# A gated DeltaNet layer on one core: adaLN slices 0 and 1 shared by two engines, and the first norms placed later in TensorE's order

## Chip, cores and metric

The kernel runs on 1 core of one Trainium2 chip. A time is the device time of one execution in microseconds (us). The kernel before takes 1131.63 us, the median of 3 runs (1130.09 to 1136.4).

## The reference

One decoder layer (DEPTH = 1) for a sequence of 1024 tokens of width 1024 in float32: adaLN modulation, a gated DeltaNet mixer, a gated residual and a last RMSNorm.

```python
mod = silu(c) @ ada_w + ada_b                       # 1024 x 3072
shift, scale, gate = split(mod, 3)
h = rms_norm(x, norm_g) * (1 + scale) + shift
proj = h @ w_in                                     # q, k, v, z, beta, a
q, k, v = silu(causal_conv4(proj_qkv))              # then q, k normalised per head
# per chunk of 64 tokens and head: A = strict_lower(beta k k^T * decay); T = (A + I)^-1
# u = T (v beta), w = T (k beta exp(gc)); a scan over the chunks carries the state
o = rms_norm(o, norm_w) * silu(z)
out = rms_norm(x + gate * (o @ w_out), final_g)
```

16 value heads share 8 query/key heads; a head has 128 channels. The kernel works with chunks of 128 tokens and 8 groups of two value heads.

## The kernel before

**Prologue (L356 to L418).** x comes in 8 row tiles. For each, ScalarE sums squares (`x_stat`), VectorE scales by the inverse norm (`x_scale`), TensorE transposes (`x_turn`, two halves of four blocks) and ScalarE or VectorE copies the result out of PSUM into `xT`: VectorE, but for the first half of the tiles in `EV_ACT`. The adaLN shift and scale are made in 8 slices of 128 channels. `ada_load(i)` brings slice i of `ada_w` (k = 0 to 7, shift and scale, two DMAs of 512 KB). Of the eight k, `ada(i)` (L233) adds up the first `KV[i]` on VectorE, one operation of 256 elements for each; `modulate(i)` (L245) does the rest on TensorE as matmuls with one moving column (L250) and folds in the accumulator with a matmul against ones (L253). With `KV[i] = 0` everything is TensorE's. Then VectorE makes the columns shift and scale (L254 to L257), ScalarE applies them to the slice's 128 rows of `xT` in two halves (L260) and makes the high part (L262), and GpSimd makes the low part (L263). Each float32 product is made of three products of high and low parts.

`first_w` and `first_lo` load and split three weight tiles: 0 is k of head 0, 1 is q of head 0, 2 is the beta and a columns. `first_project(i, j, hf)` adds channel slice i of weight tile j for token half hf into its own PSUM bank; the list `units` holds what is still to be done and `drain(n)` does n of it. `keep_warm(n)` issues n matmuls of constants.

The order of TensorE, VectorE, ScalarE and GpSimd is written out by hand in the prologue (`manual_schedule`). SP issues the DMAs of x, `ada_w` and the weights.

**Groups (L947 and on).** From here only TensorE's order is given by hand; the others' order is a planner's. `drive` mixes streams (generators that yield a cost and a delay until they are due again, in ns of a virtual clock) with filler (projection matmuls at `MM` = 216 each): a stream that is due goes first, otherwise one filler matmul is issued; when the filler is used up, the clock jumps to the next due time. Before group 0 (`gi = -1`) the streams are `gates` (second part, due at `D_G`), `stage_a(0)` (due at `START`) and `norms(1)` (due at `START1`). The filler is `proj_kq(1)`, 96 matmuls, and `values(0)` with three z heads, 240 more. `stage_a(0)` first runs `norms(0)`: for each token half transposes of k and q (L508, L515) into the two banks of tag `tr`, whose squares ScalarE sums in place (L512, L518), with `D_N` between the halves. After a delay `D_A0` follow eight Gram matmuls (L549), `D_A` apart; VectorE makes the matrices `at` from them (L551, L553). They go through DRAM into `ua`, VectorE solves 32 x 32 blocks in 31 steps (L575, L577), the result goes through DRAM into `TT`, VectorE transposes blocks of it (L597 to L599), and `levels` joins them in four TensorE steps (L603, L613, L622, L628), due `D_L0` after the Gram matmuls. Then group 0 begins with its scan.

Of the kernel before, what the change touches and what calls it, by code (L numbers as in the profile page):

```python
# [9 lines left out]
F32 = mybir.dt.float32  # L10
# [3 lines left out]
ALU = mybir.AluOpType  # L14
# [6 lines left out]

XB, WB = 8, 3
WA0 = 7
EV_ACT = (0, 1, 3, 5)
KV = (0, 0, 6, 6, 6, 6, 6, 7)
WARM = 14
PRE = (3, 5)
ND, ND0 = 3, 2

# [6 lines left out]
TURN = 40  # L36
MM = 216

START, START1 = 11000, 65000
D_G, D_RG = 9500, 11000  # L40
D_N, D_A0, D_A = 3000, 1500, 1000
D_L0, D_L1, D_L2, D_L3 = 46000, 1600, 1800, 1600
D_R, D_V, D_S = 500, 1100, 700
D_F0, D_F = 8000, 2000
# [3 lines left out]
def gdn_layer(ctx: ExitStack, tc: tile.TileContext, x, c, ada_w, ada_b, norm_g, w_in, conv_w, a_log, dt_bias,  # L48
# [8 lines left out]
    nc = tc.nc  # L57
# [7 lines left out]
    NHALF = T // TH  # L65
# [119 lines left out]
    def keep_warm(n):  # L185

        warm = bank("tr")
        for _ in range(n):
            nc.tensor.matmul(warm[:, :P], lhsT=ones, rhs=ident, start=True, stop=True)
# [26 lines left out]
    def ada_load(i):  # L216
        wa = q0.tile([P, KT, 2, P], F32, name="wa", tag="wa", bufs=WB)
        for s in range(2):
            nc.sync.dma_start(out=wa[:, :, s], in_=av[:, :, s, i])
        was[i] = wa  # L220
# [12 lines left out]
    def ada(i):  # L233

        wa, n = was[i], KV[i]
        if n == 0:
# [27 lines left out]
                                    h_hi[hf][i // 4][:, i % 4].bitcast(F32), op=ALU.subtract)  # L264

    first = [(8 * P, P), (0, P), (BA0, 2 * HV)]
    w0, acc0 = [], []

    v3 = lambda a: a.rearrange("p (n h) -> p n h", h=HV)

# [50 lines left out]
        yield 650, 0  # L321

    GENG = {nc.tensor.engine, nc.vector.engine}
    raw0 = []
    dtb = const.tile([P, HV], F32, name="dtb")
    nea = const.tile([P, HV], F32, name="nea")
    nc.scalar.dma_start(out=dtb, in_=dt_bias[0:1, :].to_broadcast([P, HV]))
# [2 lines left out]
    def first_w(j, load=False):  # L330
        c0, m = first[j]
        if load:
            raw = q0.tile([P, D], F32, name="w0raw", tag="xt", bufs=XB)[:, :KT * m].rearrange("p (k n) -> p k n", n=m)
            nc.sync.dma_start(out=raw, in_=wv[:, :, c0:c0 + m])
            raw0.append(raw)
            return
        both = q0.tile([P, KT, 2, m], F32R, name=f"w0{j}")
        nc.scalar.copy(both[:, :, 0], raw0[j])
        w0.append(both)

    def first_lo(j):
        hi, lo = w0[j][:, :, 0], w0[j][:, :, 1]
        nc.vector.tensor_tensor(lo, raw0[j], hi.bitcast(F32), op=ALU.subtract)
        w0[j] = (hi, lo) if j < 2 else w0[j].rearrange("p k s m -> p k (s m)")

    def first_project(i, j, hf):
# [10 lines left out]
    with tc.manual_schedule(engines={nc.tensor.engine, nc.vector.engine, nc.scalar.engine, nc.gpsimd.engine}):  # L357
# [3 lines left out]
        for t in range(NT):  # L361
            x_load(t)
            if t == WA0:
                ada_load(0)
        for j in range(3):
            first_w(j, True)
        for i in (1, 2):
            ada_load(i)
        for t in range(3):
            x_stat(t)  # L370
        x_scale(0)
        for t in range(NT):
# [6 lines left out]
                columns()  # L379
            if t + 3 < NT:  # L380
                x_stat(t + 3)
        first_w(1)
        first_w(2)
        first_lo(0)
        modulate(0)
        keep_warm(WARM)
        first_lo(1)
        first_lo(2)
        units = []

        def drain(n):
# [3 lines left out]
        for i in range(KT):  # L395
            if i + 3 < KT:
                ada_load(i + 3)
            if i > 0:
                drain(ND)
                if i + 1 < KT:  # L400
                    modulate(i + 1)
                if i + 2 < KT:
                    ada(i + 2)
                drain(1)
            for hf in range(NHALF):
                first_project(i, 2, hf)
            units += [(i, j, hf) for hf in range(NHALF) for j in range(2)]
            if i == 0:
                drain(ND0)
                modulate(1)  # L410
                ada(2)
                nc.scalar.activation(nea, nea, AF.Exp)
            if i in PRE:
                c0 = (9, 1)[PRE.index(i)] * P
                ahead[c0] = load_w(c0, P, wpool)
# [118 lines left out]
    def stage_a(gi, G):  # L534
# [3 lines left out]
            yield from norms(gi, G)  # L538
        D1 = dram.tile([16, P, 32], F32, name="D1", tag="D1", bufs=2)
        D2 = dram.tile([16, 4, 16, 2, 32], F32, name="D2", tag="D2", bufs=2)  # L540
        yield 0, D_A0
        for hf in range(NHALF):
            em, brk = G.em[hf], G.brk[hf]

# [491 lines left out]
```

## Time and profile before

| | us |
|---|---|
| median of 3 runs | 1131.63 |
| profiled execution | 1130.95 |
| its span | 1129.2 |

| engine | busy us | share of the span |
|---|---|---|
| TensorE (PE) | 1059.3 | 94% |
| weight loads (PEld) | 857.6 | 76% |
| VectorE (DVE) | 745.1 | 66% |
| ScalarE (ACT) | 536.6 | 48% |
| GpSimd (POOL) | 450.0 | 40% |

A busy share is an average over stages. Matmuls are pipelined and their ends are modelled, so a busy TensorE may be at half clock or running one-column matmuls; the granted clock (PEclk, 1.00 is 2.4 GHz and 0.50 is 1.2 GHz) tells one of the two, the forms in the timeline the other. A wait in brackets is idle time of the engine before the piece, with what ended it.

### The profile page before, as it was taken

The numbers are of one execution on the slowest core, as the hardware profiler recorded it, in microseconds if no ns is written. First come the engines' busy times: TensorE is split into PE (matmuls) and PEld (weight loads), VectorE is DVE, ScalarE is ACT, GpSimd is POOL, SyncE is SP. The second block draws the span as 40 slices with busy tenths as digits, with TensorE's granted clock in tenths as the row PEclk, the third lists the DMA queues.
The fourth block names the chain that finished last, engine by engine and source line by source line (L and its number), as shares of the span: only waits on it lengthen the run. The fifth ranks groups of instructions, "written<-read, shape, count | busy, mean of one in ns | idle before, by whom it ended". The sixth has DMA issues, their size and how long they took to land.

```text
span 1129.2 us, 18338 instructions
## 1 busy us (share of the span) xinstructions
PE 1059.3 (94%) x6295; PEld 857.6 (76%) x6295; DVE 745.1 (66%) x1914; ACT 536.6 (48%) x1416; POOL 450.0 (40%) x532
## 2 busy tenths in 40 slices
PE   8997999989999799999999999999899989999997
PEld 7875787767878678777877887788678768778785
DVE  5468775776579857865786677677766866513515
ACT  6567442453642455435543644364546424534523
POOL 3452223532444135323532452155216334954643
PEclk9998999999999999999999999999999989999999
DMA  9803333341145313421531143125313571446442
GB/s 287 234 19 133 75 82 85 101 126 43 39 135 164 83 50 100 125 56 30 145 102 45 42 146 84 39 54 163 74 29 103 149 219 63 140 135 185 152 121 75
DMA packets 188131, 119.48 MB, mean 106 GB/s; under 512 B 59733, under 2 KB 166534, under 8 KB 187014
## 3 DMA queue, kind: packets, MB, share of 16 engines
q1 hardware_dynamic: 187536, 118.20, 37.2%
q8 instruction: 50, 0.82, 0.3%
q14 instruction: 43, 0.35, 0.1%
q10 hardware_dynamic: 502, 0.10, 0.0%
HBM read 93.03 MB, written 25.24 MB: 105 GB/s over the span
## 4 chain that ended last, share of the span: by engine, by line
PE 41%; DVE 18%; ACT 6%; POOL 5%; DMA 4%; issue 4%; SPq 0%; POOLq 0%; DVEq 0%; ACTq 0%
PE pj L459 16%; PE pj L837 5%; DVE tb L577 4%; DVE tm L575 4%; DVE vT L446 3%; DVE em L497 3%; PE tr L549 2%; PE tr L837 2%; PE ts L755 2%; PE ks L736 1%; PE oq L709 1%; PE oq L762 1%; PE tr L622 1%; PE ks L767 1%; PE tr L628 1%
## 5 line engine op out<-in xcount | busy, mean ns | idle before, releaser
L124 POOL TENSOR_TENSOR wlo<-wraw,whi 128x512 fp32r<-128x512 f32 x92 | 126.1, 1379 | 147.3 <-ACT whi L123 107.7
L446 DVE SCALAR_TENSOR_TENSOR vT<-xb,taps,vT 128x512 f32<-128x512 f32 x96 | 84.6, 882 | 24.3 <-ACT vT L444 23.3
L446 DVE SCALAR_TENSOR_TENSOR kq<-xb,taps,kq 128x512 f32<-128x512 f32 x96 | 78.7, 828 | 12.9 <-ACT kq L444 11.0
L123 ACT CAST whi<-wraw 128x512 fp32r<-128x512 f32 x92 | 55.5, 618 | 64.9 <-PE pj L459 59.0
L577 DVE TENSOR_TENSOR tb<-tb,tm 128x126 f32<-128x126 f32 (+22 forms) x248 | 80.1, 323 | 4.8
L698 POOL TENSOR_TENSOR oT<-oT,z 128x256 f32<-128x256 f32 x64 | 50.6, 792 | 81.2 <-ACT oT L697 74.0
L575 DVE TENSOR_TENSOR tm<-tb,ua 128x126 f32<-128x126 f32 (+22 forms) x248 | 78.3, 316 | 6.2 <-DMA ua<-D 1.1
L459 PE MATMUL pj<-h1hia,whi 128*128 128x512 f32 x184 | 75.8, 412 | 6.6 <-ACT vT L444 6.6
L697 ACT ACTIVATE oT<-pot,cols 128x256 f32<-128x256 f32 x64 | 30.4, 474 | 108.1 <-PE pot L695 54.8
L459 PE MATMUL pj<-h0lob,whi 128*128 128x512 f32 x184 | 78.2, 425 | 0.0
L459 PE MATMUL pj<-h0hia,whi 128*128 128x512 f32 x184 | 76.8, 417 | 1.3 <-ACT kq L444 1.3
L459 PE MATMUL pj<-h1hib,whi 128*128 128x512 f32 x184 | 77.8, 423 | 0.0
L459 PE MATMUL pj<-h1lob,whi 128*128 128x512 f32 x184 | 77.7, 422 | 0.0
L459 PE MATMUL pj<-h1hia,wlo 128*128 128x512 f32 x184 | 77.5, 421 | 0.0
L459 PE MATMUL pj<-h0hib,wlo 128*128 128x512 f32 x184 | 77.1, 419 | 0.0
L459 PE MATMUL pj<-h1hib,wlo 128*128 128x512 f32 x184 | 76.6, 416 | 0.0
L459 PE MATMUL pj<-h0hia,wlo 128*128 128x512 f32 x184 | 75.8, 412 | 0.0
L459 PE MATMUL pj<-h1loa,whi 128*128 128x512 f32 x184 | 75.7, 411 | 0.0
L459 PE MATMUL pj<-h0loa,whi 128*128 128x512 f32 x184 | 75.6, 411 | 0.0
L459 PE MATMUL pj<-h0hib,whi 128*128 128x512 f32 x184 | 75.5, 410 | 0.0
L439 POOL MEMSET xb<- 128x3 f32 x32 | 3.4, 109 | 172.3 <-DVE kq L446 85.9
L719 POOL TENSOR_TENSOR sso<-sso,neg_half 128x2 f32<-128x2 f32 x64 | 44.6, 696 | 58.3 <-DVE sso L718 57.6
(445 smaller groups left out, 2933.1 us busy)
## 6 DMA issues: line engine op xcount, KB each, us to landing
wraw<-in_gdn_w_in SPq DMA_DIRECT2D x92, 256.0 KB, 2.9
woraw<-in_gdn_w_out SPq DMA_DIRECT2D x54, 256.0 KB, 3.2
wa<-in_ada_w SPq DMA_DIRECT2D x16, 512.0 KB, 6.9
em<-gc_dram SPq DMA_DIRECT2D x8, 1024.0 KB, 6.4
z_dram<-sz SPq DMA_DIRECT2D x32, 256.0 KB, 2.1
z<-z_dram SPq DMA_DIRECT2D x64, 128.0 KB, 2.4
o_dram<-oT SPq DMA_DIRECT2D x64, 128.0 KB, 1.9
gsrc<-o_dram SPq DMA_DIRECT2D x32, 256.0 KB, 2.9
```

The lines of the kernel that those rows point to most:

```text
L123: nc.scalar.copy(hi, raw)
L124: nc.gpsimd.tensor_tensor(lo, raw, hi.bitcast(F32), op=ALU.subtract)
L446: nc.vector.scalar_tensor_tensor(dst, xb[:, j:j + TH], tp[:, j], dst, op0=ALU.mult, op1=ALU.add)
L459: nc.tensor.matmul(ps[:m], lhsT=a[:, k, :m], rhs=b[half][k // 4][:, k % 4], start=(k == 0 and n == 0), stop=(k == KT - 1 and n == 2))
L497: nc.vector.scalar_tensor_tensor(em[:, h, n], em[:, h, n], ngc[:, n, h0 + h:h0 + h + 1], mask, op0=ALU.add, op1=ALU.add)
L549: nc.tensor.matmul(pg2[:, 0:2], lhsT=kq[hf][:, 0, js], rhs=kq[hf][:, :, js], start=True, stop=True)
L575: nc.vector.tensor_tensor(tmv, tb[:, :mm, j:j + 1].to_broadcast([P, mm, ln]), ua[:, j:j + 1, j + 1:].to_broadcast([P, mm, ln]), op=ALU.mult)
L577: nc.vector.tensor_tensor(tb[:, :mm, j + 1:], tb[:, :mm, j + 1:], tmv, op=ALU.subtract)
L697: nc.scalar.mul(oT, pot, normw_c)
L698: nc.gpsimd.tensor_tensor(oT, oT, zs.pop(n), op=ALU.mult)
L719: nc.gpsimd.tensor_tensor(sso, sso, neg_half[:, :2], op=ALU.pow)
L837: nc.tensor.matmul(acc, lhsT=a[:, ts], rhs=b, start=(first and n == 0), stop=(last and n == 2))
```

## The change

Constants: three k of slice 0 and five k of slice 1 go to VectorE (none before), slices 2 to 6 give it seven instead of six; the first halves of x tiles 6 and 7 are copied by ScalarE; the warm-up behind slice 0 has 10 matmuls instead of 14; `D_G` goes from 9500 to 11000, `START` from 11000 to 16000, and group 0 alone gets a `D_A0` of 6000 instead of 1500. Order: weight tile 1 (q) is loaded behind slice 1 of `ada_w`; `ada(0)` stands before `modulate(0)`, `first_lo` of tiles 0 and 2 behind it, then `ada(1)`, and tile 1 is split last, its low part by GpSimd; `units` lists both halves of k before those of q.

```diff
-EV_ACT = (0, 1, 3, 5)
-KV = (0, 0, 6, 6, 6, 6, 6, 7)
-WARM = 14
+EV_ACT = (0, 1, 3, 5, 6, 7)
+KV = (3, 5, 7, 7, 7, 7, 7, 7)
+WARM = 10
...
-START, START1 = 11000, 65000
-D_G, D_RG = 9500, 11000
-D_N, D_A0, D_A = 3000, 1500, 1000
+START, START1 = 16000, 65000
+D_G, D_RG = 11000, 11000
+D_N, D_A0, D_A = 3000, (6000, 1500), 1000
...
-        nc.vector.tensor_tensor(lo, raw0[j], hi.bitcast(F32), op=ALU.subtract)
+        (nc.gpsimd if j == 1 else nc.vector).tensor_tensor(lo, raw0[j], hi.bitcast(F32), op=ALU.subtract)
...
-        for j in range(3):
+        for j in (0, 2):
             first_w(j, True)
-        for i in (1, 2):
-            ada_load(i)
+        ada_load(1)
+        first_w(1, True)
+        ada_load(2)
...
-        first_w(1)
+        ada(0)
         first_w(2)
-        first_lo(0)
         modulate(0)
         keep_warm(WARM)
+        first_lo(0)
+        first_lo(2)
+        ada(1)
+        first_w(1)
         first_lo(1)
-        first_lo(2)
...
-            units += [(i, j, hf) for hf in range(NHALF) for j in range(2)]
+            units += [(i, j, hf) for j in range(2) for hf in range(NHALF)]
...
-        yield 0, D_A0
+        yield 0, D_A0[gi > 0]
```

## Rows read from the trace of the kernel before

**Rows 1.** The page's first part: busy us, share of the span, instructions.

```profile
PE 1059.3 (94%) x6295; PEld 857.6 (76%) x6295; DVE 745.1 (66%) x1914; ACT 536.6 (48%) x1416; POOL 450.0 (40%) x532
```

**Rows 2.** Stretches: length, PE, PEld, DVE, ACT, POOL busy us (instructions), PEclk, DMA share, GB/s.

```profile
20.00:30.00 10.00, 10.00 (x63) 10.00 (x62) 5.18 (x10) 5.16 (x7) 2.28 (x2) 0.66 1.18 275
...
76.00:93.50 17.50, 16.29 (x78) 13.28 (x78) 16.49 (x39) 12.72 (x21) 7.10 (x12) 1.00 0.19 50
93.50:98.20 4.70, 1.41 (x9) 0.96 (x9) 2.52 (x5) 4.67 (x22) 1.34 (x1) 0.97 0.86 313
98.20:101.30 3.10, 3.10 (x9) 2.47 (x8) 2.77 (x8) 2.65 (x8) 1.40 (x2) 0.50 0.97 374
101.30:104.60 3.30, 3.30 (x15) 2.45 (x13) 3.30 (x17) 2.28 (x5) 0.00 (x0) 0.99 0.54 158
104.60:107.30 2.70, 0.17 (x1) 0.00 (x0) 2.70 (x8) 2.67 (x5) 0.10 (x1) 1.00 0.00 0
107.30:115.00 7.70, 6.90 (x17) 5.09 (x18) 4.75 (x22) 2.91 (x8) 1.05 (x1) 0.56 0.00 0
115.00:124.30 9.30, 8.56 (x38) 6.74 (x38) 8.64 (x24) 7.32 (x8) 2.80 (x2) 1.00 0.32 71
```

**Rows 3.** Timeline of TensorE, 20 to 42 us: start, length, engine, line, operation.

```profile
20.68 4.85 PE L250 MATMUL tr<-cols,wa 128*128 128x1 f32 x32
25.39 5.41 PE L189 MATMUL tr<-ident,ones 128*128 128x128 f32 x28
...
31.32 0.39 PE L354 MATMUL pot<-h1loa,w 128*32 128x512 f32 x1
...
32.95 3.63 PE L250 MATMUL tr<-cols,wa 128*128 128x1 f32 x32
```

**Rows 4.** Timeline of TensorE, 92 to 108 us: two projections five apart, and two waits.

```profile
92.15 0.40 PE L459 MATMUL pj<-h0hia,wlo 128*128 128x512 f32 x1
...
93.32 0.40 PE L459 MATMUL pj<-h0lob,whi 128*128 128x512 f32 x1
96.58 0.66 PE L508 MATMUL tr<-ident,kq 128*128 128x128 f32 x4 [2.87 <-ACT tr L512]
...
107.31 0.70 PE L549 MATMUL tr<-kq 128*128 128x256 f32 x2 [2.54 <-ACT tr L512]
```

**Rows 5.** Groups by line, 0 to 80 us: busy us, mean ns of one, idle before.

```profile
L242 DVE SCALAR_TENSOR_TENSOR tr<-wa,cols,tr 128x256 f32<-128x256 f32 x25 | 12.2, 490 | 0.9
```

**Rows 6.** Timeline of VectorE and GpSimd, 20 to 31 us: last copy of x, last `h_lo`.

```profile
21.34 0.68 DVE L214 COPY xT<-oq 128x512 f32<-128x512 f32 x1
...
28.99 1.27 POOL L263 TENSOR_TENSOR h1loa<-xT,h1hia 128x512 fp32r<-128x512 f32 x1
```

**Rows 7.** Timeline, 36 to 67 us: shifts of slices 1, 2, 6, 7, and slice 7's fold.

```profile
36.61 0.16 DVE L254 TENSOR_TENSOR shift_c<-tr,cols 128x1 f32<-128x1 f32 x1 [9.09 <-PE tr L250]
...
41.26 0.16 DVE L254 TENSOR_TENSOR shift_c<-tr,cols 128x1 f32<-128x1 f32 x1 [1.15 <-PE tr L253]
...
61.10 0.16 DVE L254 TENSOR_TENSOR shift_c<-tr,cols 128x1 f32<-128x1 f32 x1 [1.15 <-PE tr L253]
...
65.18 0.38 PE L253 MATMUL tr<-ones,accs 128*128 128x1 f32 x2 [0.20 <-DVE accs L242]
...
66.05 0.16 DVE L254 TENSOR_TENSOR shift_c<-tr,cols 128x1 f32<-128x1 f32 x1 [0.92 <-PE tr L253]
```

**Rows 8.** Timeline, 124 to 182 us: last `at`, solve's start, transposes, first and last level.

```profile
124.00 0.61 DVE L551 SCALAR_TENSOR_TENSOR at<-tr,brk,em 128x128 f32<-128x128 f32 x2 [0.40 <-PE tr L549]
...
135.43 0.18 DVE L575 TENSOR_TENSOR tm<-tb,ua 128x31 f32<-128x31 f32 x1
...
169.27 0.44 DVE L599 STREAM_TRANSPOSE TE<-TT 32x256 f32<-32x256 f32 x1
...
174.78 0.21 PE L603 MATMUL tr<-TE,at 32*32 32x32 f32 x1
...
181.73 1.14 PE L628 MATMUL tr<-TT,pn 64*64 64x64 f32 x16 [0.68 <-ACT pn L625]
```

More of the change, by code (lines that the diff above doesn't have):

```diff
@@ L266, in gdn_layer @@
     first = [(8 * P, P), (0, P), (BA0, 2 * HV)]
-    w0, acc0 = [], []
+    w0, acc0 = {}, []
     v3 = lambda a: a.rearrange("p (n h) -> p n h", h=HV)
@@ L323, in gdn_layer @@
     GENG = {nc.tensor.engine, nc.vector.engine}
-    raw0 = []
+    raw0 = {}
     dtb = const.tile([P, HV], F32, name="dtb")
@@ L334, in first_w @@
             nc.sync.dma_start(out=raw, in_=wv[:, :, c0:c0 + m])
-            raw0.append(raw)
+            raw0[j] = raw
             return
@@ L338, in first_w @@
         nc.scalar.copy(both[:, :, 0], raw0[j])
-        w0.append(both)
+        w0[j] = both
     def first_lo(j):
         hi, lo = w0[j][:, :, 0], w0[j][:, :, 1]
-        nc.vector.tensor_tensor(lo, raw0[j], hi.bitcast(F32), op=ALU.subtract)
+        (nc.gpsimd if j == 1 else nc.vector).tensor_tensor(lo, raw0[j], hi.bitcast(F32), op=ALU.subtract)
         w0[j] = (hi, lo) if j < 2 else w0[j].rearrange("p k s m -> p k (s m)")
```

## The prediction

> **What bounds the kernel now.** I read the page first: TensorE is busy for 94% of the span [rows 1], so a gain has to come from a stretch where TensorE stands still, runs at half clock, or does work that another engine can take. The page's forty slices put the weak ones into the first 200 us, so I cut those into stretches [rows 2]. There are two. From 20 to 30 us TensorE counts as busy, but the granted clock is 0.66 and what it runs is one-column matmuls and warm-up [rows 3]. From 93.5 to 124.3 us it is idle for 3.3 + 2.5 + 0.8 + 0.7 = 7.3 us (stretch less busy time) and at half clock (1.2 of 2.4 GHz) in two stretches, 3.1 us at 0.50 and 6.9 busy us at 0.56, which cost 3.1 x 0.50 + 6.9 x 0.44 = 4.6 us [rows 2]. Together 11.9 us. The timeline names the waits: the transposes of the second half of norms(0) start 2.87 us late and the first Gram matmul of `stage_a` 2.54 us late, both for the squares (L512) on ScalarE that free a `tr` bank [rows 4]. Half clock follows both waits. The change touches just these two stretches; behind about 200 us it changes nothing but the start.
>
> **Slice 0 (L233 to L257).** Now 16 matmuls of one column, two entries each in the trace, 32 in 4.85 us [rows 3]; afterwards 10 for k = 3 to 7 and 2 that fold in the accumulator, 24 entries. VectorE gets three operations of 256 elements at 0.49 us [rows 5]. It ends its copies of x at 21.34 + 0.68 = 22.0 [rows 6]; the two moved copies shorten that only to about 21.6, since the last transposes end near 20.84. The accumulator is thus there at 21.6 + 1.5 = 23.1. By then TensorE has its first 10 entries behind it and waits; 14 entries are left. At the warm-up's 5.41/28 = 0.19 us each (half clock) they end at 25.8, at slice 1's 3.63/32 = 0.113 us at 24.7, against 25.5 now [rows 3]. The clock has fallen in this stretch in the present kernel too, so I take 25.8: a loss of 0.3 us, with a gain of 0.8 as the other end. The copies of x on ScalarE stand in its wait for the weights and cost nothing there.
>
> **Warm-up and first projection.** WARM 14 to 10 takes 8 entries x 0.19 = 1.5 us from TensorE, but the fourth projection needs the second `h_lo` of slice 0, which GpSimd ends at 28.99 + 1.27 = 30.26 [rows 6]. That entry stands at 31.32 now; about 0.5 us can be had.
>
> **Slice 1.** 16 matmuls become 8, 32 entries become 16: 16 x 0.113 = 1.8 us less. Its five VectorE operations (2.5 us) fit behind the `first_lo` calls while TensorE warms up. The load of slice 1 moves ahead of a 512 KB load, so it lands sooner; that load (the q weights) lands later, but the unit order now asks for q after both k halves, and its low part goes to GpSimd, 2 x 1.27 = 2.5 us by the `h_lo` rows, behind which nothing waits before the next `h_hi`. If that cover is gone, it costs up to 2.5 us once. Slice 1's shift therefore comes at 36.61 - 2.0 = 34.6 us [rows 7].
>
> **Slices 2 to 6.** Each gives one more k to VectorE: 4 entries less, 0.45 us of TensorE for 0.49 us of VectorE, five times. One would book 2.3 us. But the present slice 7 already has seven k on VectorE, and there the loop from one shift to the next takes 66.05 - 61.10 = 4.95 us while TensorE waits for the accumulator [rows 7]: VectorE's chain is the limit. The present five loops from slice 2 to 7 take 66.05 - 41.26 = 24.8 us, 4.96 each. So the 2.3 us are worth about nothing. Slice 2's shift comes at 34.6 + 4.95 = 39.55, against 41.26: 1.7 us gained, and TensorE then waits some 2 us for slice 2's accumulator. The trace shows half clock after waits of 2.54 and 2.87 us [rows 2, 4]; here it would cost at most 0.6 us, as the loop has slack. **Prologue: 1.6 us gained, between 0 and 3.**
>
> The Trainium skill, "TensorE: Matmul & The Clock Gate", section "HAM oscillation — how this bites in real kernels", speaks against putting a wait in front of TensorE here: gaps make the clock fall. The two waits above agree, in that the clock fell behind them; by the rule the new wait before slice 2 would bring a half-clock stretch like that from 98.2 to 101.3, and the sum would come out up to 1.5 us higher, near 1124.
>
> **Gates, norms and Gram matmuls.** D_G, START and D_A0 place steps between 336 projection matmuls (proj_kq(1), values, three z heads), 0.234 us apart at full clock (1.17 us for five, [rows 4]). Adding up the driver's costs by hand: gates stand behind 44 of these now and 51 afterwards, the two halves of norms(0) behind 48 and 62, then 72 and 86, the eight Gram matmuls from 83 to 118, then from 128 to 161. TensorE thus has 72 matmuls (17 us) instead of 48 before it needs ScalarE's Silu of `kq`, and 42 instead of 21 (9.8 against 4.9 us) between the second transposes and the first Gram matmul. Both waits ended within 3 us, so both should close. VectorE is the doubt: it is busy all of 101.3 to 107.3 and 8.64 of the 9.3 us from 115 [rows 2], and two more convolutions now come to it before the Gram matmuls. I leave 2 us of the 11.9 lost (0 as the good end, 5 as the bad one).
>
> **What is late next.** The solve. The last `at` now stands at 124.6; the inputs of the level matmuls are ready 45.1 us later (169.71), and TensorE comes to them at 174.78, with 5 us to spare [rows 8]. Afterwards the last `at` is 43 matmuls and one turn, 10.4 us, later in the order: 124.6 - 11.9 - 1.6 + 2 + 10.4 = 123.5. The 45.1 us hold some 4 us in which VectorE did convolutions before it began the solve at 135.43; I keep half of them: ready at 166.5. And the levels lose their filler: now 15 projections stand between their steps (174.78 to about 182.8, 8.0 us, 3.5 of them filler [rows 8]); afterwards all 336 go first and the four steps run alone. That costs between 4.5 us (8.0 less the filler) and 8.0; I take 6.5, since each step waits for the copy of the one before, so filler and steps cost 10.0 instead of 8.0. TensorE's end of the levels: 182.8 - 11.9 + 2 + 2.0 - 1.6 = 173.3, so it reaches them at 166.8, just behind the solve's 166.5. Gain at that point: 182.8 - 173.3 = 9.5 us. From there on the order is as before, and I let 9 us through to the end.
>
> **Sum.** Profiled execution 1130.95 us (span 1129.2 and 1.75 around it) - 9.0 = 1122; the median of the runs is 0.7 above the profiled one, so 1122.5. With no stalls left and the best prologue (12 to 13 us) 1118; with 5 us of stalls and a full 45.1 us chain the levels end near 178, a gain near 5, 1126.
>
> **Rivals.**
> 1. *VectorE bounds the solve.* With TensorE no longer stopping, the same VectorE work of about 41 us up to 124.3 and two convolutions more (some 4.5 us) must fit into fewer us. If the last `at` comes 4 to 8 us later than I say, every one of them is a wait at L603, since no projection is left to hide it. Gain 1 to 5 us: 1126 to 1131. For it: VectorE's share in [rows 2]. Against: part of its work there (`em` of group 1, the gate's slices) is not wanted before the solve. Chance 0.20.
> 2. *The stalls stay and the solve only moves back: slower.* If ScalarE's order, not the room, made the stalls, 11.9 us remain and `at` comes at 124.6 - 1.6 + 10.4 = 133.4, the solve at 178.5. TensorE comes to L603 at 174.78 + 3.5 - 1.6 = 176.7, waits, and ends the levels at 185.0: +2.2 us, and with half clock behind the wait and a few us of further slip 1134 to 1140. It decides from the point where the solve is ready after 176.3 (end of levels after 182.8). For it: ScalarE was idle only briefly from 93.5 to 98.2 (4.67 of 4.70 busy). Against: the Exp and table loads in front of those squares have then been passed. Chance 0.12, two thirds of it above 1137.
> 3. *Given back in group 0.* The head gets shorter, but VectorE work that was hidden in it moves into the first scan, which has waits of its own: 1126 to 1132. Nothing in the rows is for it but VectorE's load. Chance 0.08.
>
> **How the numbers follow.** Forecast (1117 to 1126) 0.60, rivals 0.20, 0.12, 0.08. A range from 1116 to 1132 leaves out rival 2 and a little of the good end. About 0.5% (5.7 us, below 1126.0 or above 1137.3) is what a measurement of this kernel can tell from no change: faster 0.64 (the forecast and the good edge of rivals 1 and 3), same 0.28 (the rest of these two and a third of rival 2), slower 0.08.
>
> **What would show it.** Slice 1's loads with 16 entries in one run and the shift of slice 1 near 34.6; the waits of L253 for `accs` from slice 2 on with loops of 4.95 us; the first projection after the prologue 1.6 us earlier; no wait over 1 us before L508 and L549 and clock 1.00 from 90 to 120; L603 behind the last z projection near 167 and TensorE with gaps between L603, L613, L622 and L628. I am wrong if L603 waits for the transposes (L599) by several us, if L508 still waits for L512, or if the span after the levels grows.

## The result and the profile after

The changed kernel takes 1140.67 us (median, 1132.45 to 1146.6); the kernel before, run beside it, takes 1132.22. The ratio is 1.0056, 95% interval 1.0032 to 1.0081: slower by some 6 us by the ratio (the medians are 8.5 us apart), where 9 us faster had been forecast, and outside the range. The profiled execution of the changed kernel, 1132.69 us with a span of 1131.0, lies near the lower end of its own times; a second profile of the same kernel (below) has a span of 1139.2. From line 391 on, the changed kernel's lines stand 3 behind those of the rows before: L446 is now L449, L497 L500, L549 L552, L551 L554, L599 L602, L603 L606, L628 L631, L755 L758.

**Ahead of 76 us** the forecast came true in this profile. VectorE's timeline, the shifts of slices 0, 1, 2, 3 and 7 (start, length, engine, line, operation, idle before it and what ended it):

```profile
24.65 0.16 DVE L254 TENSOR_TENSOR shift_c<-tr,cols 128x1 f32<-128x1 f32 x1 [1.81 <-PE tr L253]
32.95 0.16 DVE L254 TENSOR_TENSOR shift_c<-tr,cols 128x1 f32<-128x1 f32 x1 [3.49 <-PE tr L253]
37.90 0.16 DVE L254 TENSOR_TENSOR shift_c<-tr,cols 128x1 f32<-128x1 f32 x1 [0.92 <-PE tr L253]
43.31 0.16 DVE L254 TENSOR_TENSOR shift_c<-tr,cols 128x1 f32<-128x1 f32 x1 [1.39 <-PE tr L253]
...
63.64 0.16 DVE L254 TENSOR_TENSOR shift_c<-tr,cols 128x1 f32<-128x1 f32 x1 [0.92 <-PE tr L253]
```

Against [rows 7]: slice 1 at 32.95 in place of 36.61, slice 2 at 37.90 in place of 41.26, slice 7 at 63.64 in place of 66.05. The loops are 4.95 us, as VectorE's chain wants, but for two of 5.41 (37.90 to 43.31) and 5.47 us; so of the 3.4 us that slice 2 is earlier, 2.4 are left at slice 7. The first projection behind the prologue starts at 74.80, 2.4 us earlier than before (77.21). That is the best case: in the 14 other profiles below with this prologue it stands between 74.94 and 77.92, in the middle at 75.9, and with the old prologue a second time (a) at 76.75. So the profiles give the prologue rather 1.1 us.

**From 87 to 124 us** the old waits are gone and new ones stand in their place. The stretches (length, busy us of PE, PEld, DVE, ACT, POOL with instructions, granted clock, DMA share, GB/s), to be held against [rows 2]:

```profile
75.00:87.00 12.00, 11.97 (x51) 9.30 (x50) 11.86 (x30) 7.87 (x14) 2.86 (x9) 1.00 0.15 42
87.00:90.00 3.00, 0.03 (x1) 0.06 (x1) 3.00 (x6) 1.74 (x3) 0.10 (x1) 0.93 0.00 0
90.00:93.00 3.00, 3.00 (x11) 2.80 (x12) 1.90 (x5) 0.93 (x3) 0.00 (x0) 0.50 0.33 84
93.00:112.00 19.00, 19.00 (x90) 15.30 (x89) 14.21 (x46) 16.46 (x50) 7.18 (x7) 1.00 0.65 198
112.00:124.00 12.00, 7.96 (x28) 6.13 (x27) 9.96 (x26) 6.97 (x8) 6.43 (x3) 0.86 0.08 22
124.00:175.30 51.30, 50.27 (x233) 40.10 (x232) 35.18 (x102) 16.92 (x55) 13.00 (x14) 1.00 0.37 96
175.30:185.00 9.70, 6.52 (x130) 5.85 (x129) 3.69 (x8) 2.59 (x5) 2.53 (x2) 0.66 0.37 107
185.00:189.00 4.00, 4.00 (x41) 3.11 (x42) 1.03 (x3) 1.00 (x3) 0.00 (x0) 0.55 0.00 0
```

TensorE is whole from 93 to 112, where it stood still twice before. But it stands still for 3 us at 87 and for 4 us behind 115, and from 175 to 189, in the levels and behind them, the clock is 0.66 and 0.55. In the kernel before, the stretches from 175 to 185 and from 185 to 189 had 0.91 and 0.79, and the half clock in them lay behind the levels: from its first L603 to the end of L628 (174.78 to 182.87) the clock was 1.00, in the changed kernel from L606 to the end of L631 (175.28 to 183.98) it was 0.68.

The waits in TensorE's timeline:

```profile
86.57 0.40 PE L462 MATMUL pj<-h0hia,wlo 128*128 128x512 f32 x1
89.97 0.77 PE L310 MATMUL ts<-triu,gh 128*128 128x128 f32 x2 [3.00 <-DVE gh L309]
...
112.27 0.59 PE L552 MATMUL tr<-kq 128*128 128x256 f32 x2
113.86 0.59 PE L552 MATMUL tr<-kq 128*128 128x256 f32 x2
119.66 0.67 PE L552 MATMUL tr<-kq 128*128 128x256 f32 x2 [4.04 <-DVE em L556]
```

and what VectorE did meanwhile:

```profile
84.24 5.38 DVE L449 SCALAR_TENSOR_TENSOR kq<-xb,taps,kq 128x512 f32<-128x512 f32 x8
89.54 0.28 DVE L309 COPY gh<-gt 128x128 f32<-128x128 f32 x1
...
109.92 3.50 DVE L500 SCALAR_TENSOR_TENSOR em<-em,ngc,mask 128x128 f32<-128x128 f32 x13
113.33 0.74 DVE L449 SCALAR_TENSOR_TENSOR kq<-xb,taps,kq 128x512 f32<-128x512 f32 x1
...
116.25 0.74 DVE L449 SCALAR_TENSOR_TENSOR vT<-xb,taps,vT 128x512 f32<-128x512 f32 x1
116.91 0.34 DVE L554 SCALAR_TENSOR_TENSOR at<-tr,brk,em 128x128 f32<-128x128 f32 x1
...
131.47 0.61 DVE L554 SCALAR_TENSOR_TENSOR at<-tr,brk,em 128x128 f32<-128x128 f32 x2
143.89 0.18 DVE L578 TENSOR_TENSOR tm<-tb,ua 128x31 f32<-128x31 f32 x1
...
171.84 0.44 DVE L602 STREAM_TRANSPOSE TE<-TT 32x256 f32<-32x256 f32 x1 [0.19 <-DMA TT<-D]
```

The reader sees the same thing twice. `gh`, one copy of 0.28 us for which the gates wait, stands behind eight convolution steps of 5.38 us. And at 112.27 TensorE has its first Gram matmul done, but VectorE is at `em` of *group 1*, 13 steps in 3.50 us, and then at five convolution steps; the first `at` of group 0 comes at 116.91. Both `tr` banks are full by then, and TensorE waits 4.04 us. The last `at` ends at 132.1, against 124.6 before [rows 8].

**The levels.** TensorE:

```profile
175.28 0.21 PE L606 MATMUL tr<-TE,at 32*32 32x32 f32 x1
...
179.39 1.94 PE L625 MATMUL tr<-TE,at 64*64 64x64 f32 x16 [1.49 <-DVE TE L622]
182.01 1.97 PE L631 MATMUL tr<-TT,pn 64*64 64x64 f32 x16 [0.68 <-ACT pn L628]
184.90 1.22 PE L758 MATMUL ts<-vtok,TT 128*128 128x128 f32 x4
```

L606 doesn't wait: the transposes end at 172.3, 3 us earlier. It comes at 175.28, 0.5 us later than before, since all of the filler now goes first and ends there. The four steps then run alone, the matmuls of L631 at 1.97 us where they took 1.14 [rows 8], and the first matmul of the scan stands at 184.90, against 183.65. Behind it lie 945.6 us before and 946.1 now.

### The profile page after: what moved, and what is told of

Read it like the earlier page. It is cut to its first block, busy times and chain, and to the rows that moved or that the text cites. A ratio compares the mean times of both kernels' runs of the same rounds, so it can differ in the third digit from the quotient of the medians.

```text
span 1131.0 us, 18249 instructions
## 1 busy us (share of the span) xinstructions
PE 1054.3 (93%) x6243; PEld 853.0 (75%) x6243; DVE 749.1 (66%) x1924; ACT 534.8 (47%) x1416; POOL 455.3 (40%) x533
## 4 chain that ended last, share of the span: by engine, by line
PE 36%; DVE 18%; POOL 6%; issue 6%; ACT 6%; DMA 5%; SPq 1%; POOLq 0%; DVEq 0%; ACTq 0%
PE pj L462 16%; DVE tb L580 4%; DVE tm L578 4%; PE pj L840 4%; DVE vT L449 3%; DVE em L500 3%; POOL wolo L124 2%; PE tr L552 2%; PE ks L739 2%; PE ts L758 1%; PE oq L712 1%; PE ks L770 1%; PE tr L625 1%; PE oq L765 1%; DMA woraw<-in_gdn_w_out 1%
## 5 line engine op out<-in xcount | busy, mean ns | idle before, releaser
L124 POOL TENSOR_TENSOR wlo<-wraw,whi 128x512 fp32r<-128x512 f32 x92 | 130.3, 1425 | 144.9 <-ACT whi L123 114.2
L449 DVE SCALAR_TENSOR_TENSOR vT<-xb,taps,vT 128x512 f32<-128x512 f32 x96 | 86.1, 897 | 23.9 <-ACT vT L447 22.9
L449 DVE SCALAR_TENSOR_TENSOR kq<-xb,taps,kq 128x512 f32<-128x512 f32 x96 | 77.8, 819 | 12.6 <-ACT kq L447 10.8
L462 PE MATMUL pj<-h1loa,whi 128*128 128x512 f32 x184 | 75.9, 412 | 0.0
```

The costliest lines, as they stand in the source:

```text
L124: nc.gpsimd.tensor_tensor(lo, raw, hi.bitcast(F32), op=ALU.subtract)
L449: nc.vector.scalar_tensor_tensor(dst, xb[:, j:j + TH], tp[:, j], dst, op0=ALU.mult, op1=ALU.add)
L462: nc.tensor.matmul(ps[:m], lhsT=a[:, k, :m], rhs=b[half][k // 4][:, k % 4], start=(k == 0 and n == 0), stop=(k == KT - 1 and n == 2))
```

## The experiments

The runs form four comparisons, each with the kernel before on the same chip: c, a, b, d; then e, f, g, h; then i, j, m, k; then n, q and h again. A ratio is that to the kernel before in its own comparison. A difference between two ratios carries both intervals, some 0.3% or 3 us. What I counted on: (Q) VectorE's order makes the new waits; (L) the levels lost the projections between them; (N) the gates' wait alone is the loss; and, as the first question, whether the prologue or the three constants of the driver lose the time. "Projections" in the table are those that TensorE runs between the first L606 and the first L631. In before, b, e, h and q the longest wait at L552 (L549 in before and a) is for ScalarE, in the others for VectorE. In the kernels with `em` held back (j, k, m, n, q) L500 stands at L502, L552 at L554, L602 at L605, L606 at L609, L758 at L761.

| kernel | ratio, 95% interval | wait at L310 | longest wait at L552 | projections | wait at L606 | first scan matmul |
|---|---|---|---|---|---|---|
| before | 1 | none | 2.54 | 15 | none | 183.65 |
| changed | 1.0056 (1.0032 to 1.0081) | 3.00 | 4.04 | 0 | none | 184.90 |
| c_after_again | 1.0020 (1.0000 to 1.0040) | 2.99 | 4.05 | 0 | none | 186.99 |
| a_drive_only | 1.0053 (1.0029 to 1.0077) | 3.35 | 4.04 | 0 | none | 187.93 |
| b_prologue_only | 0.9977 (0.9959 to 0.9996) | none | 2.53 | 15 | none | 180.34 |
| d_gates_early | 1.0011 (0.9988 to 1.0034) | none | 4.36 | 0 | none | 182.40 |
| e_start_only | 1.0009 (0.9987 to 1.0031) | none | 2.72 | 0 | none | 182.50 |
| f_da0_only | 1.0007 (0.9985 to 1.0029) | none | 3.90 | 0 | none | 181.74 |
| g_dg_only | 1.0003 (0.9978 to 1.0029) | 2.99 | 3.50 | 12 | none | 182.26 |
| h_levels_early | 0.9970 (0.9946 to 0.9994) | none | 2.53 | 25 | none | 180.94 |
| h_again | 0.9969 (0.9945 to 0.9994) | none | 2.53 | 25 | none | 180.12 |
| i_after_levels | 0.9997 (0.9975 to 1.0019) | 2.98 | 4.04 | 14 | none | 182.60 |
| j_after_em_late | 1.0020 (0.9998 to 1.0043) | 2.99 | 0.87 | 0 | 0.63 | 181.94 |
| m_after_all | 0.9998 (0.9981 to 1.0015) | none | 1.27 | 14 | 4.26 | 182.42 |
| k_between | 1.0042 (1.0024 to 1.0060) | none | 3.23 | 25 | 5.30 | 186.63 |
| n_all_load_kept | 0.9929 (0.9906 to 0.9953) | none | 1.27 | 14 | none | 175.42 |
| q_held_old_start | 1.0012 (0.9985 to 1.0039) | none | 2.78 | 25 | 0.82 | 186.42 |

The first scan matmul also moves with the prologue, which differs from profile to profile. Counted from the first projection behind the prologue instead, it comes 106.4 us later in the kernel before, 110.1 and 110.8 in the changed one (c), 111.2 in a, 104.2 in b, 107.0 in d, 106.3, 106.6 and 106.0 in e, f and g, 105.3 and 105.2 in h, 106.8 in i, 107.0 in j, 106.4 in m, 110.6 in k, 99.7 in n and 108.5 in q. The two kernels with two profiles agree to 0.7 and 0.1 us in this.

### Which half of the change loses the time

c_after_again is the changed kernel unaltered. a_drive_only is the kernel before with the three constants alone, b_prologue_only the changed kernel with the constants of before, d_gates_early the changed kernel with D_G of before:

```diff
 a:
-START, START1 = 11000, 65000
-D_G, D_RG = 9500, 11000
-D_N, D_A0, D_A = 3000, 1500, 1000
+START, START1 = 16000, 65000
+D_G, D_RG = 11000, 11000
+D_N, D_A0, D_A = 3000, (6000, 1500), 1000
 b: the reverse of these three lines, in the changed kernel
 d, in the changed kernel:
-D_G, D_RG = 11000, 11000
+D_G, D_RG = 9500, 11000
```

> The changed kernel unaltered, for a second profile and more times beside the parts. Theory 1 (the steps behind the prologue lose, by waits and by half clock behind them): median 1138 to 1142, the profile with other half-clock stretches than the first one, all between 75 and 200 us. Theory 2 (the prologue's new wait before slice 2 loses): the same median, the additional half clock between 20 and 75 us. Theory 3 (half clock in stretches that the change does not touch): the additional half clock behind 200 us.

> The kernel before with START, D_G and D_A0 of the change alone. Theory 1: slower than before by 5 to 12 us, with a wait of 2 to 4 us before the gate matmuls and one of 3 to 5 us among the Gram matmuls. Theory 2: within 3 us of before, or faster. My forecast would have had about 7 us faster.

> The change with START, D_G and D_A0 of before. Theory 1: 1 to 4 us faster than before, since the shift of slice 7 comes 2.4 us earlier and the rest is as before. Theory 2: 5 to 10 us slower than before.

> The changed kernel with D_G back at 9500, so that the gate matmuls are due 7 projections sooner; the planner then puts the copy that they wait for (L309) ahead of six convolution operations on VectorE. Theory 1: the 3.0 us wait before L310 goes (below 0.5 us) and with it the half clock of 90 to 93 us: 3 to 6 us faster than the changed kernel. Theory 2 or 3: within 2 us of the changed kernel.

Measured: 1136.24, 1140.78, 1130.63 and 1134.76 us beside 1133.79 of the kernel before. The constants alone lose 0.53%, some 6 us; the prologue alone gains 0.23%, 2.6 us. That settles the half: the whole loss is in three numbers of the driver, and the prologue gains, by an amount inside its forecast of 0 to 3 us. b's profile has 1.1 us of the gain at the first projection (76.15); 2.2 more come behind it, where nothing but the start was changed: from 93.5 to 124.3 us it has 2.5 us of half clock (busy time times what the clock lacked, stretch by stretch) in place of 4.6. The changed kernel itself is nearer to the kernel before here (0.2%) than in the first comparison (0.56%). Its second profile has the two waits of the first to 0.01 us, but reaches the scan 2.1 us later, 1.4 of them there at the first projection, and needs 952.2 us in place of 946.1 for what lies behind. d takes the gates' wait away and is only 1.5 us below c, where theory 1 had 3 to 6:

```profile
85.78 0.38 PE L310 MATMUL ts<-triu,gh 128*128 128x128 f32 x2
98.47 0.66 PE L511 MATMUL tr<-ident,kq 128*128 128x128 f32 x4 [0.96 <-ACT tr L515]
117.18 1.19 PE L552 MATMUL tr<-kq 128*128 128x256 f32 x2 [4.36 <-DVE em L556]
```

L310 comes without a wait, but TensorE is then earlier at the Gram matmuls and waits longer there (4.36 in place of 4.04), and the wait at L511 is partly back. That speaks against theory N, though d's time alone, with an interval of 0.23% to either side, can't rule out a gain of 3 us; that e and f below lose as much as g, without any wait of the gates, does the rest.

### Each constant alone

Three kernels put one constant each into b (START 16000; D_A0 (6000, 1500); D_G 11000). A fourth leaves the constants as in b and makes the levels of group 0 due earlier:

```diff
 h, in b:
-D_L0, D_L1, D_L2, D_L3 = 46000, 1600, 1800, 1600
+D_L0, D_L1, D_L2, D_L3 = (42000, 46000), 1600, 1800, 1600
...
-        yield 0, D_L0
+        yield 0, D_L0[gi > 0]
```

> The new prologue with one of the three constants of the change: START 16000, the gates' and the Gram step's delays as before. Theory Q (the cost is VectorE's order: all of em of group 1 stands ahead of the first at): the first L552 waits 3 to 4.5 us for VectorE, half clock behind it, last at after 127; median 1133 to 1136 against 1130.6 of the prologue alone. Theory L (the cost is the levels that fall behind the filler: START moves their place in the planned order 15 projection matmuls later, 15 x 0.233 = 3.5 us, so that none of the 15 between the first L606 and the last L631 is left): the stretch from the first L606 to the first scan matmul has no projection in it, 9 us or more at half clock; 1133 to 1136 as well, but then D_A0 alone costs the same. Rival N (the gate wait L310 alone is the cost): 1130 to 1131.

> The new prologue with D_A0 (6000, 1500) alone. Theory Q: em of group 1 is ahead of the first at here too, but the Gram matmuls stand 4.5 us later in the order, so their wait is at most 1 us; median within 1 us of the prologue alone (1130 to 1132). Theory L: the levels stand 15 projections later, as with START alone, none left between them: 1133 to 1136. Rival N: 1130 to 1131.

> The new prologue with D_G 11000 alone. Rival N (the gate wait is what the constants cost): L310 waits 3 us for gh behind the convolution steps of VectorE, half clock for 3 us behind it, 4 to 5 us: 1134 to 1136. Theory L: 12 of the 15 projections stay between the levels, so 0.7 us at the levels; with a gate wait of 3 us that is only 3 us in all: 1132.5 to 1134. Theory Q: the at steps come ahead of em of group 1, so the Gram matmuls wait under 0.5 us.

> The new prologue with the constants of before, and in group 0 alone the levels due 4 us earlier (D_L0 42000 in place of 46000): 25 projections between the first L606 and the last L631 in place of 15. Theory L: the levels' own time is hidden further, 10 x 0.233 = 2.3 us off the stretch, less what L606 waits for the solve (ready at 167.6 in the profile of the prologue alone, L606 then at 167): 2 to 3 us faster than the prologue alone, 1127.5 to 1129. Theories Q and N: no change, 1130 to 1131. If the solve is later than 168 the wait takes the gain: 1130 to 1132.

Measured: 1133.27, 1131.74, 1132.25 and 1128.51 beside 1131.12. Against b's ratio, which is from another chip, each constant alone costs 0.26 to 0.32%, about 3 us, with intervals of the same size: e and f are just clear of none, g isn't. The profiles agree, with 106.0 to 106.6 us from the first projection to the scan in place of b's 104.2; so each costs some 2 us there, and none is the whole. e is at the lower end of its two theories, g just under its own, and f, at 1131.74, came out where theory Q had it (1130 to 1132) and not at L's 1133 to 1136. But the reason that Q gave for that time is wrong: with D_A0 alone the Gram matmul still waits 3.90 us, where Q gave at most 1 us for it, so pushing the Gram step back doesn't help it: VectorE does all of `em` of group 1 first there too. And g waits 3.50 us there, where Q had under 0.5, with all of `em` of group 1 behind the first `at`: with the gates late (L310 at 91.42 in place of 86.52), `em` of *group 0* starts at 101.95 in place of 97.12 in b, and the first `at` comes at 110.61 in place of 107.81. So `em` of group 1 is not the only VectorE work that holds `at` up. The two constants that leave no projection between the levels give this from 175 to 185 (e, then f):

```profile
175.00:185.00 10.00, 7.83 (x102) 6.89 (x96) 3.68 (x8) 2.21 (x5) 1.26 (x1) 0.55 0.27 79
...
175.00:185.00 10.00, 7.83 (x118) 6.59 (x118) 3.68 (x8) 2.21 (x5) 1.26 (x1) 0.66 0.27 81
```

and h, with 25 projections between them, this from L606 past the end of L631 (177.27) and the first scan matmul (180.12; from its second run):

```profile
165.80:181.00 15.20, 13.87 (x169) 10.79 (x169) 6.23 (x12) 3.10 (x6) 4.16 (x4) 1.00 0.32 98
```

From the first to the last level matmul the clock is 0.68 in e and 0.84 in f, with 0.50 from there to the scan; with 15 projections in between (before, b) or 25 (h) it is 1.00. So theory L holds for the clock. h is faster than both kernels, twice, at 0.997; against b its gain (0.0007) is within the interval, below the 2 to 3 us that I had given it, and its first scan matmul is no earlier than b's (180.94 and 180.12 against 180.34): ten projections more between the steps show no gain.

### The new losses taken out of the changed kernel

i gives the changed kernel its projections back between the levels, with a due time as much earlier as START and D_A0 are later (5 + 4.5 us). j holds `em` of group 1 back until the last `at` of group 0 has been written. m does both and has D_G of before. k puts j's edit into b, with constants between old and new.

```diff
 i, in the changed kernel:
+D_L0, D_L1, D_L2, D_L3 = (36500, 46000), 1600, 1800, 1600
 j, in norms, ahead of the load of em:
+        if gi == 1:
+            nc.vector.tensor_copy(em[:, 0, 0, 0:1], Gs[0].at_last[:, 7, 0:1])
 k, in b, with j's edit:
+START, START1 = 13000, 65000
+D_N, D_A0, D_A = 3000, (2500, 1500), 1000
+D_L0, D_L1, D_L2, D_L3 = (39500, 46000), 1600, 1800, 1600
```

> The changed kernel with the levels of group 0 due 9.5 us earlier (D_L0 36500 there), so that 14 projections stand again between the first L606 and the last L631, as 15 did before. Theory L: their cover was what the change lost at its end; 14 x 0.233 = 3.3 us less at most 1 us in which L606 waits for the solve (ready at 172.3 in the profile of the changed kernel), and less half clock behind 175: 3 to 5 us faster than the changed kernel, which is level with the kernel before (ratio 0.998 to 1.002 where the changed kernel had 1.002 to 1.0056). Theory Q: the waits at L310 and L552 are all of the loss, and the levels, waiting for the solve, give nothing: within 1 us of the changed kernel.

> The changed kernel with em of group 1 held back until the last at of group 0 (a copy of one element from at into em ahead of its load; nothing else is altered). Theory Q: the wait of 4.04 us at the first L552 and those of 0.39 and 0.64 behind it go, with the half clock behind the first; filler ends 4 us or more earlier, and as the solve too starts 4 us earlier nothing is given back: 4 to 6 us faster than the changed kernel, ratio to the kernel before 0.997 to 1.001. Rival: VectorE comes no earlier to the first at, since the convolution steps ahead of it remain (4 of them, 2.7 us): wait 2 to 3 us, 1 to 2 us faster. Theory L: what is gained before the filler's end is kept, since the levels stand behind the filler in any case.

> The changed kernel with all three of its new losses undone at once and its START and D_A0 kept: gates due at 9500, em of group 1 held back, levels of group 0 due 9.5 us earlier. If the three are the whole loss: no wait at L310, at most 0.5 us at the first Gram matmuls, and the gain of the prologue (3 us) and of the old waits (5 us) shows at last: 1122 to 1127, ratio 0.992 to 0.997. Rival: the solve, 6 us later than before by START and D_A0, now comes after the filler's end and the levels wait for it: the first of the levels' matmuls waits 3 to 5 us, 1128 to 1131. Rival: half clock in stages that nothing here touches takes the gain: same waits gone, but over 1130.

> The new prologue with constants between the old and the new: START 13000, D_G 9500, D_A0 2500 for group 0, em of group 1 held back, levels of group 0 due at 39500. The solve is ready 2 to 3 us later than with the old constants (167.6 then, about 170 here) and the waits at the first L511 (2.50) and the first L552 (2.53, for ScalarE) are halved. Expected 1124 to 1128, ratio 0.993 to 0.997, faster than both kernels; if the wait at L511 stays at 2.5 and the levels wait for the solve, 1128 to 1130, as with the levels alone moved.

Measured: 1130.95, 1133.27, 1130.72 and 1136.29 beside 1131.42. i does what was expected: level with the kernel before, though both waits are still there, so the levels were 0.23% (against c, within the intervals) to 0.59% (against the first comparison, clear of them) of the time, 3 to 7 us; from the first projection to the scan the profiles have 106.8 us for 110.1 and 110.8. j closes the wait at L552 (0.87 for 4.04) and gains nothing in time that can be told from c, though its profile comes to the scan as i's does (107.0 us). m undoes all three (1.27 us of wait are left at L554) and gains nothing over i. k, which was to beat both kernels, is the slowest but the changed one and a; it also waits 3.23 us at L554 for VectorE, which is at convolutions between the `at` steps although `em` is held back. Why m and k gain nothing stands at the levels' first matmul, in m and in k:

```profile
171.07 0.31 PE L609 MATMUL tr<-TE,at 32*32 32x32 f32 x2 [4.26 <-DVE TE L603]
...
172.10 0.28 PE L609 MATMUL tr<-TE,at 32*32 32x32 f32 x2 [5.30 <-DVE TE L603]
```

TensorE was there at 171.07 - 4.26 = 166.8 and 172.10 - 5.30 = 166.8 and waits for the solve. 166.8 is where the forecast had TensorE arrive, but with all 336 projections behind it; in m 14 of them, 3.3 us, are still to come. The solve, forecast to be ready at 166.5, is 5 us late. Here the clock falls in spite of the projections in between: 0.76 in m and 0.81 in k from the first to the last level matmul, behind waits of 4.26 and 5.30 us. One suspect for the late solve is in my own edit. The copy stands ahead of the load of `em`, so that the load waits for `at` too, and SP's queue in k shows where it then goes:

```profile
124.32 1.78 SPq L563 DMA_DIRECT2D D<-at  x4
127.58 0.39 SPq L139 DMA_DIRECT2D wraw<-in_gdn_w_in  x1
128.47 0.35 SPq L498 DMA_DIRECT2D em<-gc_dram  x1
129.06 1.16 SPq L570 DMA_DIRECT2D ua<-D  x2
```

The load of `em` is issued between the writing of `at` and its reading back as `ua`, from which the solve begins.

### The load left where it was

n is m with the copy behind the load, as a step that adds zero times `at` to the first column of each of `em`'s 16 blocks; the load's place is as in the changed kernel. q has the same in b, with the levels due at 41000. h was run once more beside them.

```diff
 n, in norms, behind the load of em:
+        if gi == 1:
+            nc.vector.scalar_tensor_tensor(em[:, :, :, 0], Gs[0].at_last[:, 7:8, 0:NT].to_broadcast([P, 2, NT]),
+                                           0.0, em[:, :, :, 0], op0=ALU.mult, op1=ALU.add)
```

> As m_after_all (gates due at 9500, levels due 9.5 us earlier, START and D_A0 of the changed kernel), but of group 1 only the 16 VectorE steps on em are held behind the last at of group 0; its load from gc_dram stays where the changed kernel has it. Theory S (in m the load, moved into the time between the last at and the reading back of ua, held the solve up): last at 126.2 as there, solve 11.5 us behind it at about 137.7 in place of 139.9, TE ready at 169 to 170, the levels' first matmul waits 2 us in place of 4.26; 1128 to 1130 against 1130.7 of m. Rival (the solve starts late because at itself is late, the load costs nothing): solve at 139.5 or later, wait over 4 us, median as m's, within 1 us.

> The new prologue, START, D_G and D_A0 of before, levels of group 0 due at 41000, and the 16 VectorE steps on em of group 1 held behind the last at of group 0, their load not moved. The at steps are then not interleaved with em: waits of 0.52 and 0.86 at L552 close, last at at 118.5 to 119.5 in place of 120.3, solve ready at about 165: if the filler and the solve then meet, 1126.5 to 1128, 1 to 2 us faster than h_levels_early; if VectorE's em steps now stretch the solve (16 x 0.3 us beside it), 1128 to 1130.

> h_levels_early unaltered, on the same chip as the two above: 1128 to 1129, ratio to the kernel before 0.996 to 0.998, its first scan matmul where it was to 1 us. What lies behind that matmul, the same instructions in every kernel here, may differ by up to 6 us between its two profiles, as it did between the two profiles of the changed kernel (946.1 and 952.2): that is half clock and not the change. If it agrees to 1 us, the difference behind that matmul belongs to the kernel.

Measured: 1125.88, 1135.93 and 1131.05 beside 1134.17. n is 0.71% faster than the kernel before, about 8 us, and the fastest of all. VectorE and TensorE in n:

```profile
125.85 0.61 DVE L556 SCALAR_TENSOR_TENSOR at<-tr,brk,em 128x128 f32<-128x128 f32 x2
...
138.27 0.18 DVE L581 TENSOR_TENSOR tm<-tb,ua 128x31 f32<-128x31 f32 x1
...
166.29 0.43 DVE L605 STREAM_TRANSPOSE TE<-TT 32x256 f32<-32x256 f32 x1
...
166.38 0.24 PE L609 MATMUL tr<-TE,at 32*32 32x32 f32 x2
...
175.42 0.71 PE L761 MATMUL ts<-vtok,TT 128*128 128x128 f32 x4 [0.15 <-DVE TT L635]
```

The load's place is worth more than theory S had, but not by the way that S named, the memory. In m the last `at` began at 126.19, the solve ran from 139.90 to 162.87 and the transposes ended at 171.94; in n they are 125.85, 138.27, 159.11 and 166.72. Of the 5.2 us, 0.3 is `at`, 1.3 the time up to the solve, 2.1 the solve itself and 1.5 the way back. The reading of `ua` is issued no later in m than in n, and VectorE waits for it in neither. SP's queue and VectorE in m, then in n:

```profile
130.28 1.17 SPq L570 DMA_DIRECT2D ua<-D  x2
134.13 0.35 DVE L502 SCALAR_TENSOR_TENSOR em<-em,ngc,mask 128x128 f32<-128x128 f32 x1 [1.45 <-DMA em<-gc_dram]
139.04 0.34 DVE L502 SCALAR_TENSOR_TENSOR em<-em,ngc,mask 128x128 f32<-128x128 f32 x1
139.90 0.17 DVE L581 TENSOR_TENSOR tm<-tb,ua 128x31 f32<-128x31 f32 x1
...
130.43 2.22 SPq L570 DMA_DIRECT2D ua<-D  x2
132.48 1.66 DVE L502 SCALAR_TENSOR_TENSOR em<-em,ngc,mask 128x128 f32<-128x128 f32 x6
```

`ua` lands by 136.6 us in m and by 135.7 in n (issue and time to landing), at least 3.3 and 2.6 us ahead of the solve, a time in which VectorE is busy with convolutions and, in m, with `em`. What the moved load did is to let `em` arrive at 134.1, so that its 16 steps stand in front of the solve (4) and inside it (12); in n all have ended at 134.2. On the way back, m's queue has two weight loads ahead of the loads of `TT` (165.38 to 167.00) and n's has none. The solve is ready as TensorE arrives, and the first scan matmul comes at 175.42, 8.2 us earlier than before.

q is a miss: the same step in b, with the levels due 1 us earlier than in h, is 0.43% slower than h, nearly 5 us. Its last `at` ends at 122.6 and its solve is ready at 168.8, where 118.5 to 119.5 and 165 were expected. It has 1.20 us of wait at the second L552 (h 0.52 and 0.66), 0.82 for the solve (h none) and 1.87 at L620 for VectorE, which was at group 1's small operations (h 1.33). Its prologue too reached the first projection at 77.92, later than any other here, with 13.5 us of half clock between 20 and 45 us where h had 7. In the profiles its first scan matmul is 5.5 and 6.3 us behind h's two; 3.3 of these are lost behind the first projection, by the step and the earlier due time together, and the rest is that prologue. h again has its first scan matmul 0.8 us from where it was, and 943.8 us behind it in place of 947.9.

## Why the prediction was wrong

**Slice 0** was 0.9 us earlier (24.65 for 25.57 before): the other end of the estimate. The clock was 1.00 from 20 to 24.5 us, where it had been 0.82 in the kernel before, and fell only in the warm-up behind (0.69 from 24.5 to 30), so the price from the half-clock row was the wrong choice. **Slice 1** at 32.95 is better than the 34.6. **Slices 2 to 6** were read rightly: 4.95 us a loop, worth nothing. The wait in front of slice 2 was 2.50 us with half clock from 38.2 to 41.5 behind it, and the loop took 5.41 us, so it cost 0.5 us, inside the 0.6. The Trainium skill ("TensorE: Matmul & The Clock Gate", "HAM oscillation — how this bites in real kernels") has the clock fall after gaps in TensorE's work, though the waits of its example are longer than this one; here it fell (0.57 from 38 to 42 us), and the loop's slack hid all of the 1.5 us but this. **The prologue**, 1.6 us by the sum, gave 2.4 in this profile, about 1.1 over all profiles, and 2.6 in b's time, with an interval of about 0.5 to 4.6.

**The step that failed is "I leave 2 us of the 11.9 lost", drawn from "both should close".** Both did close: there is no wait at L511 and none at the first L552, and 93 to 112 is whole. But the stretch lost nearly what it had lost before (11.9): from 87 to 124 there are 3.0 + 4.0 us idle and 3.0 us at 0.50 and 8.0 at 0.86 (1.5 + 1.1 us), 9.6 in all, and the last `at` was at 132.1 and not 123.5. The text counted how many projections stand ahead of each step in TensorE's order, and asked of VectorE only whether it was busy. VectorE works its own order through, and a step that is due later in the plan has its VectorE work put behind other work: `gh` behind eight convolution steps when D_G grew, `at` behind `em` of group 1 when START or D_A0 grew. Rival 1 had the right engine in the wrong place. It let every late `at` become a wait at L603; `at` was 8.6 us later than forecast and L606 did not wait at all, since the same waits had held the filler up. The doubt named there, that "part of its work there (`em` of group 1, the gate's slices) is not wanted before the solve", was taken as a point against the rival; such work standing ahead of `at` was the mechanism (j: the wait falls from 4.04 to 0.87 us once `em` is held back).

**The solve, "ready at 166.5"**, was ready at 172.3 in the changed kernel and at 166.7 in n. The 40.2 us from the last `at` (43 were forecast) were less than thought; the solve itself took 20.8 us in place of 26.6.

**The levels alone**, taken at 6.5 us, between 4.5 and 8.0, took 8.7 (175.28 to 183.98). The bounds held the chain of copies but not the clock. With no projection between the steps it fell to 0.66 and stayed at 0.55 behind them, here over the stretches from 175.3 and 175 to 185 and from 185 to 189: 6.52 x 0.34 + 4.0 x 0.45 = 4.0 us of half clock against 9.25 x 0.09 + 4.0 x 0.21 = 1.7 us before. i shows that the missing projections were worth 3 to 7 us; the clock within the levels was 1.00 with 14, 15 or 25 projections between the steps (n and i, before and b, h), 0.93 with 12 (g) and 0.68 to 0.84 with none, but m and k had 0.76 and 0.81 with 14 and 25, behind their waits.

**The sum** has two ends rounded down: from 1131.65 us (1130.95 and 0.7) a gain of 13 gives 1118.7 and one of 5 gives 1126.7. **The gain** was to be 9.5 us at the levels, and the forecast "let 9 us through to the end". The profiled execution is 1.3 us behind at the first scan matmul, the second profile of the same kernel 3.3 us, and the rest of the program needs 0.5 or 6.6 us more. The second part is not explained by the change: a profile from each of two runs of one kernel differs by 6.1 us there (c against the first) or by 4.1 (h). The forecast had no term for that. So of the 6 us that the first comparison shows, the two profiles place 1.3 to 3.3 ahead of the scan; where the rest lies stays open.

**Rival 2** named the sign and about the price (1134 to 1140; 1140.67 and, in c, 1136.24 were measured), but by stalls that stay; they went. Its point, the solve ready later than TensorE arrives, is what stopped m and k, and cost j 0.63 us. With the three new losses undone (n) the forecast's gain comes out: 8.2 us at the scan (9.5 forecast), 0.71% (0.8). That its times come out too is in part luck: TensorE is at the first level matmul at 166.4 (166.8), but with 14 projections still to come, and the levels with them take 8.3 us for the 6.5; the solve is ready at 166.7 (166.5), but from an `at` that ended at 126.5 and not 123.5, with 40.3 us behind it and not 43. So the gain was possible, but one of the three constants had to be taken back and two things done that the change did not do. That the loss of the changed kernel is these three and nothing else is shown within the spread of about 4 us that the comparisons have; c and the first comparison differ by 0.36% for the same kernel.

## What to carry to other kernels

Where a plan sets due times for one engine, moving a step later moves its feeders on the other engines as well: look up what now stands ahead of the one small operation for which the step waits (`gh`, `at`), not only how much filler there is. Due times hang together: START and D_A0 grew by 9.5 us, and as the levels' own delay stayed, the levels fell out of their filler; taking that delay back by the same 9.5 us made the loss good, within 0.2%. When a step is held back, hold the arithmetic and leave its load where it is: the same three edits came to 0.02% with the load moved behind the hold (m), so that the arithmetic came when its data came, in the middle of the solve, and to 0.71% without (n).

## What the runs showed of the hardware

The granted clock in the levels went with the work between the small matmuls and with the wait ahead of them: from the first to the last of them it was 0.68 to 0.84 with no projection in between (seven profiles), TensorE being idle for 3 to 4 us of 8 to 9.5, and 1.00 with 14 (n, i), 15 (before, b) or 25 (h), though TensorE was idle there too, for 0.7 to 1.3 us. Where a wait of 4.26 or 5.30 us stood in front (m, k), it was 0.76 and 0.81 in spite of 14 and 25 projections, and in q, with 25 and waits of 0.82 and 1.87 us, 0.88. Which of the two, the small matmuls or the gaps between them, lets it fall was not taken apart. n:

```profile
166.40:176.00 9.60, 8.61 (x148) 6.92 (x148) 4.23 (x10) 3.17 (x6) 2.53 (x2) 1.00 0.52 146
```

What I had not expected is how much the clock varies in code that is the same. Two profiles of the changed kernel from 350 to 450 us, the first and c:

```profile
350.00:450.00 100.00, 91.84 (x598) 73.96 (x597) 76.09 (x213) 47.70 (x136) 34.63 (x45) 0.98 0.34 88
...
350.00:450.00 100.00, 91.66 (x576) 72.51 (x575) 78.07 (x220) 43.22 (x119) 30.80 (x39) 0.95 0.32 86
```

It was 0.98 and 0.95 there, and likewise from 850 to 950 us, at nearly the same busy time: 4 and 10 us at half clock in each. Whether the start of these stretches, the chip or chance decides was not settled.
